# Issue order at three stage boundaries, and two steps from the sink attention's scores to its transposes

## The chip, the cores and the metric

The kernel runs on one core of a Trainium2 chip. The metric is the device time of one execution in microseconds (us), the median of a few runs. A core has five engines that each work through their own queue of instructions in order: TensorE (PE, with its weight loads as PEld), VectorE (DVE), ScalarE (ACT), GpSimd (POOL) and SyncE (SP). In this kernel SP issues the DMA transfers, so SP's queue is also the order in which loads and stores start.

## The reference

Three residual blocks over a sequence of 1024 tokens of width 1024, one after the other, all in f32.

```python
# block 1: dilated attention (3 groups of 8 heads) and an RWKV-7 recurrence side by side
proj = rms_norm(x, pre_norm_gain) @ w_in
y_attn = (o_attn * silu(z_attn)) @ w_up_attn
y_rwkv = (o_rwkv * silu(z_rwkv)) @ w_up_rwkv
merged = sigmoid(g_attn) * y_attn + sigmoid(g_rwkv) * y_rwkv
x1 = x + rms_norm(merged @ w_out, post_norm_gain)
# block 2: gMLP
u, v, z = split(rms_norm(x1, a_pre_g) @ a_w_in, 3)           # 2048 columns each
s = einsum('gts,bnsgc->bntgc', causal(w_s), layer_norm(gelu(v))) + b_s   # per 128-token chunk
x2 = x1 + rms_norm((gelu(u) * s * silu(z)) @ a_w_out, a_post_g)
# block 3: sliding-window attention, 16 query heads, 4 key/value heads, a sink in each softmax
kv_in = rms_norm(x2, kv_norm_g);  k = kv_in @ w_k;  v = kv_in @ w_v
q, z = split(rms_norm(x2, b_pre_g) @ b_w_in, 2)
m = maximum(max(logits + alibi), sink)
o = exp(logits - m) @ v / (sum(exp(logits - m)) + exp(sink - m))
out = x2 + rms_norm((o * silu(z)) @ b_w_out, b_post_g)
```

## The kernel before

**Products.** Each f32 operand is cut into a high and a low part (`whi`, `wlo`, `Ahi`, `Alo`: ACT copies the high part, DVE subtracts to get the low one), and a product is three products of such parts, summed in a bank of PSUM. A bank holds 128 x 512 f32. There are two pools of banks for this: `pd` has 2 slots, and `pb` (taken by `bank()`, `psP` too) has 6. A product that takes a slot waits until the slot's last user has been evacuated, that is, read by DVE or ACT.

**Order.** The order of the instructions on every engine is the order in which the program emits them (`manual_schedule`). A `tick` is called after every fourth matmul, and once more at a group's end. At a tick three things happen (`tick`): stores that were put on the list `late` with a count of ticks go out when the count of the list's head is used up (`store`, `flush`; the list is first in, first out); the weight planner (`w_step`) loads and splits weights as far as tiles are free; and each lane, a queue of generators, takes its next step, where `yield n` means that the next step comes n ticks on. `drain` and loops of the form `while ...: lane.step()` take steps at once.

**Phase 1 and 1a** compute block 1's projection, dilated attention (items of `att_unit`) and RWKV. **Phase 2**, the merge (`phase2`, `gated`), has 32 groups of 12 matmuls of 128 x 512: 16 on the RWKV branch (`or_hi`, `or_lo`), then 16 on the attention branch (`oa_hi`, `oa_lo`). Group n needs the gated activations of its half, which `gated` prepares: load `oa` and `ob`, multiply on DVE after 5 ticks (L1468), copy the high part on ACT (L1470), subtract on DVE (L1472). All 32 groups write to `pd`. Their evacuation is a DVE multiplication by a gate that is loaded two groups ahead (L1521).

**out_proj** is the output product with its residual, used as `w_out`, `a_out` and `b_out`. For each half of the tokens and each half c of the columns it keeps four banks, two of `pd` and then two of `pb`, as `ps[0]` to `ps[3]`, evacuated by ACT (L1635) and DVE (L1636). Afterwards `norm`, on lane `lane_n`, makes the residual sum, hands it to `store` with 3 ticks, and prepares the next block's activations.

**Phase 3** is block 2. Its products alternate between a bank of `pb` (`psP`) and one of `pd` (L1947). In the last round (`ct == 15`), after the third product, it flushes the late stores and sets up `a_out`, whose activations `stream` loads back from DRAM (`yraw<-Y`) and splits. `jit` starts the next split at a tick, as far as `jit_limit` allows; `jit_limit` 2 is set right there.

**Phase 4** is block 3. `swa_prep`, first on `lane_w`, issues the loads of the mask (`swa`), the slopes and, in four transfers, the sinks, and after 20 ticks lets POOL negate the sinks. The groups of v, k and the first two of q follow, then 14 more groups, q and z by turns, while `lane_a` runs the attention. An item of the attention is one of four steps d of a unit p:

- Q: score products (PE, L978)
- S: scores with bias and row minimum (DVE, L996), sinks (L1001), exponentials on ACT (L1008, L1011); scores go to the tiles `Sx`, exponentials to other tiles `P`
- norm: DVE adds the sink's term, inverts and scales P (L1022, L1024, L1028); only with sinks
- B: transposes of P on PE (L1042), copied by ACT (L1056 to L1058)
- C: products with V (L1077)

In a step of `att_unit`, C of the item two back comes first, then Q of the new item, B of the item before, S of the new one; 2 ticks later norm of the new one, and 3 ticks later the next step. Evacuations of a z group (`ev_z`) wait in the program until its unit's output is there (`while p not in self.Oh: self.lane_a.step()`), then emit `tz` on ACT (L2112), `tz` on DVE (L2113, L2114) and the split `yb` (L1495, L1496).

Of the kernel before, what the change touches and what calls it, by code (L numbers as in the profile page):

```python
# [129 lines left out]
class Core:  # L130
# [212 lines left out]
    def group(self, i, act, KT, half, evac, off=0):  # L343

        w = self.w_get(i)
        ps = self.pd.tile([128, 512], F32, tag="pd", name="pd")

        def op(k):
            wh, wl = w(k)
            ah, al = act(k, half)  # L350
            return wh[:, off:off + 128], wl[:, off:off + 128], ah, al
        self.mm(ps, KT, op)
        evac(ps, half)
        self.tick()
# [524 lines left out]
class Attn(Rwkv):  # L879
# [105 lines left out]
    def att_S(self, it):  # L985
# [4 lines left out]
        it["P"] = [self.s2("P") for _ in range(2)]  # L990
        Sx = [self.s2("Sx") for _ in range(2)]
# [22 lines left out]
    def att_norm(self, it):  # L1014

        nc = self.nc
        if "es" not in it:
            return
        es, d = it["es"], it["d"]
        e2 = es.rearrange("p (s j) -> p s j", s=2)  # L1020
        ST = it["u"]["ST"][:, 1].rearrange("p (s b) -> p s b", s=2)
        nc.vector.tensor_tensor(out=e2, in0=e2, in1=ST[:, :, 2 * d:2 * d + 2], op=ALU.add)  # L1022
        rd = self.sm.tile([128, 4], F32, tag="rd", name="rd", bufs=3)
        nc.vector.reciprocal(out=rd, in_=es)  # L1024
        for j in range(2):
            for s, c in enumerate(it["cols"][j]):
                P = it["P"][j]
                nc.vector.tensor_scalar(out=P[:, c], in0=P[:, c], scalar1=rd[:, 2 * s + j:2 * s + j + 1], scalar2=None,  # L1028
                                        op0=ALU.mult)
# [88 lines left out]
    def att_unit(self, u):  # L1118
        t = self.sm.tile([128, 32], F32, tag="ST", name="ST", bufs=3)
        u["STt"] = t  # L1120
        u["ST"] = t.rearrange("p (m s) -> p m s", m=2)
        for d in range(4):
            if len(self.pipe) > 1:
                self.att_C(self.pipe.pop(0))
            it = self.att_Q(u, d)
            if self.pipe:
                self.att_B(self.pipe[-1])
            self.att_S(it)
            self.pipe.append(it)
            yield self.pace[0]  # L1130
            self.att_norm(it)
            yield self.pace[1]

    def att_flush(self):
        while self.pipe:
            if "PT" in self.pipe[0]:
                self.att_C(self.pipe.pop(0))
            rest = [it for it in self.pipe if "PT" not in it]
            if rest:
                self.att_B(rest[0])  # L1140
            yield self.pace[0]
# [66 lines left out]
class Kernel(Attn):  # L1208
# [250 lines left out]
    def gated(self, o, sz, half, pr, h, l, x=None, done=None):  # L1459
# [7 lines left out]
        yield 5  # L1467
# [30 lines left out]
    def phase2(self):  # L1498
# [83 lines left out]
        for n in range(32):  # L1582
# [10 lines left out]
            self.group(i, act, 4, half, (ev_r if key == "r" else ev_a)(n), off=128 * (f % 2))  # L1593
# [8 lines left out]
    def out_proj(self, name, KT, post, xsrc, xdst, nxt, act):  # L1602
# [11 lines left out]
        def run(half, lanes):  # L1614
# [3 lines left out]
            for c in range(2):  # L1618
                i0 = self.first[name, half] + c * KP
                ps = [self.pd.tile([128, 512], F32, tag="pd", name="pd") for _ in range(2)] + [self.bank() for _ in range(2)]  # L1620
# [58 lines left out]
        def norm(half, og, x, ss):  # L1679
# [6 lines left out]
            for j in range(4):  # L1686
# [4 lines left out]
                self.store(xdst[128 * tt:128 * tt + 128, :], x[j], 3 if nxt is not None else 0)  # L1691
# [30 lines left out]
    def stream(self, src, KT, in_a):  # L1722
# [45 lines left out]

        self.jit = jit
# [80 lines left out]
    def phase3(self):  # L1850
# [105 lines left out]
        for ct in range(16):  # L1956
# [38 lines left out]
            self.tick()  # L1995
            c2 = add(product(i, combo("S2"), "T2"), c1)
            if ct:
                lane_s.add(spatial(ct, sp))
            if ct == 15:
                self.flush()  # L2000
                self.out2 = self.out_proj("a_out", 16, "a_post_g_2", self.X1, self.X2, "plain", self.stream(self.Y, 16, 4))
                self.jit_limit = 2
            self.tick()
# [29 lines left out]
    def swa_prep(self):  # L2033
        nc, I = self.nc, self.I
        t = self.s2("swa")
# [10 lines left out]
        yield 20  # L2046
# [144 lines left out]
```

## Time and profile before

| | |
|---|---|
| median of 3 runs | 2565.06 us (2563.25 to 2567.79) |
| profiled execution, its own time | 2560.33 us |
| its span in the trace | 2558.5 us |
| mean granted clock of TensorE | 0.984 |
| busy: PE, DVE, ACT, POOL | 96%, 49%, 39%, 23% of the span |
| DMA | 229.66 MB, mean 90 GB/s |

Times in the trace are us from the start of the span. A row of a timeline gives the start, the length and the instruction, and in brackets how long the engine had been idle and which instruction released it. `SPq` is the issue of a DMA. The granted clock is 1.00 at 2.4 GHz and 0.50 at 1.2 GHz. The profiled execution's own time holds 1.8 us that lie outside the span.

### The profile page before, as it was taken

The page shows a single profiled execution, that of the slowest core. Times are in us where ns is not written, and L with a number is a line of the kernel's source. Part 1 is how long each engine was busy: PE and PEld are TensorE (multiplying, and loading weights), DVE is VectorE, ACT ScalarE, POOL GpSimd, SP SyncE. Part 2 cuts the span into 40 slices and gives each one's busy share as a digit, 9 for nine tenths or more (in the row PEclk, how much of TensorE's full clock was granted, in tenths as well). Part 3 has the DMA queues.
Part 4 walks back from the last instruction along what each step waited for, and adds up shares of the span by engine and source line. Part 5 has one row for each costly group of instructions (what it writes and reads, how often), then busy time and mean ns, then how long its engine had stood idle before and what let it go on. Part 6 is the DMA issues. An engine that isn't in the chain of part 4 may idle for free.

```text
span 2558.5 us, 39497 instructions
## 1 busy us (share of the span) xinstructions
PE 2464.2 (96%) x15058; PEld 1944.8 (76%) x15058; DVE 1262.5 (49%) x3010; ACT 1009.4 (39%) x2583; POOL 599.4 (23%) x885
## 2 busy tenths in 40 slices
PE   7999999999999999999999999999999997999998
PEld 5767777777777777777788777888877886777777
DVE  5445545453322323235647347655555546566545
ACT  4222222222244444454235232544443433466632
POOL 0161715234000102011410135544440004000000
PEclk9999999999999999999999999999999999999999
DMA  5321201111211213137734232332335544000033
GB/s 144 72 59 38 71 27 57 47 54 54 50 51 30 75 45 75 46 79 225 239 113 182 87 109 85 99 99 78 100 99 201 188 133 127 26 26 26 18 115 141
DMA packets 247666, 229.66 MB, mean 90 GB/s; under 512 B 25035, under 2 KB 188939, under 8 KB 247476
## 3 DMA queue, kind: packets, MB, share of 16 engines
q1 hardware_dynamic: 247476, 227.13, 29.1%
q8 instruction: 119, 1.95, 0.3%
q14 instruction: 71, 0.58, 0.1%
HBM read 179.61 MB, written 47.48 MB: 89 GB/s over the span
## 4 chain that ended last, share of the span: by engine, by line
PE 61%; DVE 6%; DMA 4%; ACT 4%; issue 2%; POOL 2%; SPq 0%; DVEq 0%; ACTq 0%; POOLq 0%
PE pd L336 31%; PE pb L1628 7%; PE pd L1628 7%; PE pd L1947 4%; PE psP L1947 3%; PE psO L1077 2%; PE pb L1042 2%; PE pb L978 2%; DMA vg<-Vd 2%; DVE wlo L278 1%; PE pb L1926 1%; ACT vg L1905 1%; ACT P L1008 1%; DVE wlo L1496 1%; DMA gate<-GT 1%
## 5 line engine op out<-in xcount | busy, mean ns | idle before, releaser
L336 PE MATMUL pd<-Ahi,whi 128*128 128x512 f32 x1488 | 598.8, 402 | 21.3 <-DVE K L2079 12.7
L336 PE MATMUL pd<-Ahi,wlo 128*128 128x512 f32 x1488 | 598.1, 402 | 0.7 <-DVE wlo L278 0.7
L336 PE MATMUL pd<-Alo,whi 128*128 128x512 f32 x1488 | 597.5, 402 | 0.6 <-DVE Alo L427 0.6
L336 PEld LDWEIGHTS pd<-Ahi,whi 128*128 128x128 f32 x1488 | 283.3, 190 | 84.9 <-issue 17.8
L278 DVE TENSOR_TENSOR wlo<-wraw,whi 128x512 fp32r<-128x512 f32 x380 | 270.4, 748 | 150.3 <-ACT whi L277 142.8
L336 PEld LDWEIGHTS pd<-Alo,whi 128*128 128x128 f32 x1488 | 283.1, 190 | 62.3 <-issue 4.0
L336 PEld LDWEIGHTS pd<-Ahi,wlo 128*128 128x128 f32 x1488 | 282.8, 190 | 60.8 <-issue 2.1
L277 ACT ACTIVATE whi<-wraw 128x512 fp32r<-128x512 f32 x380 | 217.2, 621 | 58.5 <-POOL wraw L271 14.3
L1008 ACT ACTIVATE P<-Sx,ST 128x192 f32<-128x192 f32 (+2 forms) x320 | 130.5, 410 | 8.2 <-DVE ST L996 4.4
L1496 DVE TENSOR_TENSOR wlo<-wraw,whi 128x512 fp32r<-128x512 f32 x96 | 82.1, 869 | 56.8 <-ACT whi L1495 56.8
L996 DVE CUSTOM_DVE_ANT_0 Sx<-pb,BT 128x64 f32<-128x64 f32 (+1 forms) x192 | 44.6, 287 | 130.7 <-PE pb L978 130.3
L336 PE MATMUL pd<-wlo,Ahi 128*128 128x512 f32 x256 | 100.5, 393 | 2.5 <-DVE wlo L278 2.5
L336 PE MATMUL pd<-whi,Ahi 128*128 128x512 f32 x256 | 100.2, 391 | 0.0
L336 PE MATMUL pd<-whi,Alo 128*128 128x512 f32 x256 | 100.1, 391 | 0.0
L723 POOL TENSOR_TENSOR X<-UC,X 128x60 f32<-128x60 f32 (+24 forms) x248 | 79.5, 320 | 57.9 <-DVE UC L716 40.0
L725 POOL TENSOR_TENSOR X<-X 128x60 f32<-128x60 f32 (+24 forms) x248 | 79.4, 320 | 19.4
L1495 ACT ACTIVATE whi<-wraw 128x512 fp32r<-128x512 f32 x96 | 59.6, 622 | 58.4 <-POOL wraw L223 54.5
L271 POOL TENSOR_TENSOR wraw<-wraw,bpg 128x1024 f32<-128x1024 f32 x16 | 31.1, 1952 | 210.6 <-DMA wraw<-in_b_w_in_dram 154.3
L1042 PE MATMUL pb<-K,P 128*128 128x128 f32 (+1 forms) x388 | 63.2, 291 | 15.4 <-DVE P L1028 15.4
L1077 PEld LDWEIGHTS psO<-PT,V 128*64 128x64 f32 x1040 | 55.1, 136 | 28.3 <-issue 21.6
L1077 PE MATMUL psO<-PT,V 128*64 128x128 f32 x1040 | 74.4, 280 | 0.0
L1905 ACT ACTIVATE vg<-vg,lnv 128x128 f32<-128x128 f32 x128 | 52.6, 482 | 47.3 <-DMA vg<-Vd 47.3
(416 smaller groups left out, 4823.8 us busy)
## 6 DMA issues: line engine op xcount, KB each, us to landing
wraw<-in_w_in_dram SPq DMA_DIRECT2D x78, 512.0 KB
wraw<-in_a_w_in_dram SPq DMA_DIRECT2D x48, 512.0 KB
wraw<-in_a_w_out_dram SPq DMA_DIRECT2D x32, 512.0 KB
GT<-gt SPq DMA_DIRECT2D x32, 256.0 KB
gate<-GT SPq DMA_DIRECT2D x32, 256.0 KB
wraw<-in_w_out_dram SPq DMA_DIRECT2D x16, 512.0 KB
X<-xr SPq DMA_DIRECT2D x16, 512.0 KB
Vd<-v SPq DMA_DIRECT2D x32, 256.0 KB
```

The source lines that it names most:

```text
L277: nc.scalar.activation(out=his[j], in_=t[:, s], func=AF.Copy)
L278: nc.vector.tensor_tensor(out=los[j], in0=t[:, s], in1=his[j].bitcast(F32), op=ALU.subtract)
L336: nc.tensor.matmul(ps, lhsT=a, rhs=b, start=(n == 0), stop=(n == last))
L723: nc.gpsimd.tensor_tensor(out=tv, in0=U[:, j:j + 1, 0:j].to_broadcast([128, w, j]), in1=X[:, b0:8, j:j + 1].to_broadcast([128, w, j]), op= ...
L725: nc.gpsimd.tensor_tensor(out=X[:, b0:8, 0:j], in0=X[:, b0:8, 0:j], in1=tv, op=ALU.add)
L1008: nc.scalar.activation(out=it["P"][j][:, c], in_=Sx[j][:, c], func=AF.Exp, scale=-1.0, bias=ST[:, 0, n:n + 1], accum_out=ST[:, 1, n:n + 1])
L1042: tr = lambda x, m=128: nc.tensor.transpose(ps[0:m, 128 * x:128 * x + 128], Pt[:, 128 * x:128 * x + m], self.ident)
L1077: nc.tensor.matmul(O(h).rearrange("p (s x) -> p s x", s=2), lhsT=V[:, b - 1 + t, c:c + 64], rhs=rhs, start=t == tiles[0], stop=t == 1)
L1496: nc.vector.tensor_tensor(out=lo, in0=src, in1=hi.bitcast(F32), op=ALU.subtract)
L1628: nc.tensor.matmul(ps[j], lhsT=a, rhs=b, start=(k == 0 and n == 0), stop=(k == KT - 1 and n == 2))
L1905: nc.scalar.activation(out=v[:, tt, :], in_=v[:, tt, :], func=AF.Identity, scale=lnv[:, tt, 1:2], bias=lnv[:, tt, 0:1])
L1947: nc.tensor.matmul(ps, lhsT=a, rhs=b, start=(n == 0), stop=(n == 11))
```

## The change

At the three boundaries between the blocks:

- **Merge** (`group`, `phase2`, `gated`): every odd group writes to a bank of `pb` (`other=True`) and not of `pd`. `gated` waits 7 ticks between its loads and its first multiplication, where it waited 5.
- **out_proj**: `ps[0]` and `ps[1]` are of `pb`, `ps[2]` and `ps[3]` of `pd`. The stores of the residual sums go out 14 ticks after they are handed over, where it was 3 (`b_out` still stores at once).
- **a_out loads** (`stream`, `phase3`): `stream` issues the first two loads when it is set up (`ahead=2`), which now comes before the third product of the last round; the flush there is gone; `jit_limit = 2` is set after the tick that follows.
- **Mask constants** (`swa_prep`): the loads of mask, slopes and sinks go out after 24 ticks; the negation follows 10 ticks later.

In the sink attention, B of an item comes two steps after its S, and not one, so that the pipe is one item longer: norm of an item is emitted in the next item's step, at the place where the new item's norm was. The exponentials are written over the scores, so that `Sx` and `P` are the same tiles. For the dilated attention, which has no sinks, the order stays, and the tiles are shared as well.

```diff
--- before.py
+++ after.py
@@ -340,10 +340,10 @@
             if after is not None:
                 after(k)
 
-    def group(self, i, act, KT, half, evac, off=0):
+    def group(self, i, act, KT, half, evac, off=0, other=False):
 
         w = self.w_get(i)
-        ps = self.pd.tile([128, 512], F32, tag="pd", name="pd")
+        ps = self.bank() if other else self.pd.tile([128, 512], F32, tag="pd", name="pd")
 
         def op(k):
             wh, wl = w(k)
@@ -987,8 +987,8 @@
         nc = self.nc
         u, d, ps = it["u"], it["d"], it.pop("ps")
         BT, ST = u["bias"], u["ST"]
-        it["P"] = [self.s2("P") for _ in range(2)]
-        Sx = [self.s2("Sx") for _ in range(2)]
+
+        it["P"] = Sx = [self.s2("P") for _ in range(2)]
         for s in range(2):
             for j in range(2):
                 c, nk = it["cols"][j][s], it["nk"][j][s]
@@ -1016,7 +1016,7 @@
         nc = self.nc
         if "es" not in it:
             return
-        es, d = it["es"], it["d"]
+        es, d = it.pop("es"), it["d"]
         e2 = es.rearrange("p (s j) -> p s j", s=2)
         ST = it["u"]["ST"][:, 1].rearrange("p (s b) -> p s b", s=2)
         nc.vector.tensor_tensor(out=e2, in0=e2, in1=ST[:, :, 2 * d:2 * d + 2], op=ALU.add)
@@ -1119,16 +1119,19 @@
         t = self.sm.tile([128, 32], F32, tag="ST", name="ST", bufs=3)
         u["STt"] = t
         u["ST"] = t.rearrange("p (m s) -> p m s", m=2)
+
+        n = 2 if "nsink" in u else 1
         for d in range(4):
-            if len(self.pipe) > 1:
+            if len(self.pipe) > n:
                 self.att_C(self.pipe.pop(0))
             it = self.att_Q(u, d)
-            if self.pipe:
-                self.att_B(self.pipe[-1])
+            if len(self.pipe) >= n:
+                self.att_B(self.pipe[-n])
             self.att_S(it)
             self.pipe.append(it)
             yield self.pace[0]
-            self.att_norm(it)
+            if n == 2 and len(self.pipe) > 1:
+                self.att_norm(self.pipe[-2])
             yield self.pace[1]
 
     def att_flush(self):
@@ -1137,6 +1140,7 @@
                 self.att_C(self.pipe.pop(0))
             rest = [it for it in self.pipe if "PT" not in it]
             if rest:
+                self.att_norm(rest[0])
                 self.att_B(rest[0])
             yield self.pace[0]
 
@@ -1464,7 +1468,7 @@
         if x is None:
             nc.sync.dma_start(a, o[pr][:, s])
         nc.sync.dma_start(b, sz[pr][:, s])
-        yield 5
+        yield 7
         nc.vector.scalar_tensor_tensor(out=a, in0=a if x is None else x[:, s], scalar=0.5, in1=b, op0=ALU.mult, op1=ALU.mult)
         yield 1
         nc.scalar.activation(out=h, in_=a, func=AF.Copy)
@@ -1590,7 +1594,7 @@
                 self.lane_g.step()
             gate(n + 2)
             i = self.first[key] + f // 2
-            self.group(i, act, 4, half, (ev_r if key == "r" else ev_a)(n), off=128 * (f % 2))
+            self.group(i, act, 4, half, (ev_r if key == "r" else ev_a)(n), off=128 * (f % 2), other=n % 2 == 1)
             if f % 2 and half:
                 self.w_free(i)
         mg_split()
@@ -1617,7 +1621,7 @@
             ss = self.sm.tile([128, 2, 4], F32, tag="oss", name="oss")
             for c in range(2):
                 i0 = self.first[name, half] + c * KP
-                ps = [self.pd.tile([128, 512], F32, tag="pd", name="pd") for _ in range(2)] + [self.bank() for _ in range(2)]
+                ps = [self.bank() for _ in range(2)] + [self.pd.tile([128, 512], F32, tag="pd", name="pd") for _ in range(2)]
 
                 def part(kp, j):
                     w = self.w_get(i0 + kp)
@@ -1688,7 +1692,7 @@
                 for h in range(2):
                     xs = x[j][:, 512 * h:512 * h + 512]
                     nc.vector.scalar_tensor_tensor(out=xs, in0=og[h, j], scalar=r[:, j:j + 1], in1=xs, op0=ALU.mult, op1=ALU.add)
-                self.store(xdst[128 * tt:128 * tt + 128, :], x[j], 3 if nxt is not None else 0)
+                self.store(xdst[128 * tt:128 * tt + 128, :], x[j], 14 if nxt is not None else 0)
                 yield 1
                 if nxt is not None:
                     for h in range(2):
@@ -1719,7 +1723,7 @@
 
         return run
 
-    def stream(self, src, KT, in_a):
+    def stream(self, src, KT, in_a, ahead=0):
 
 
 
@@ -1766,6 +1770,8 @@
                 split()
             return hl[half, k]
 
+        for _ in range(ahead):
+            load()
         self.jit = jit
         return act
 
@@ -1993,14 +1999,16 @@
             self.tick()
             c5 = copy(product(i, combo("S1"), "T1"), "c5")
             self.tick()
+            if ct == 15:
+
+                actY = self.stream(self.Y, 16, 4, 2)
+                self.out2 = self.out_proj("a_out", 16, "a_post_g_2", self.X1, self.X2, "plain", actY)
             c2 = add(product(i, combo("S2"), "T2"), c1)
             if ct:
                 lane_s.add(spatial(ct, sp))
+            self.tick()
             if ct == 15:
-                self.flush()
-                self.out2 = self.out_proj("a_out", 16, "a_post_g_2", self.X1, self.X2, "plain", self.stream(self.Y, 16, 4))
                 self.jit_limit = 2
-            self.tick()
             z0 = gate(add(product(i, block(0, 1), "B21"), c1, c1))
             u0 = self.s2("u0")
             nc.gpsimd.tensor_tensor(out=u0, in0=c2, in1=c5, op=ALU.add)
@@ -2032,6 +2040,7 @@
 
     def swa_prep(self):
         nc, I = self.nc, self.I
+        yield 24
         t = self.s2("swa")
         nc.sync.dma_start(t[:, 0:384], I["const_swa"].rearrange("p a k -> p (a k)"))
         sl = self.const.tile([128, 2, 8], F32, name="slope")
@@ -2043,7 +2052,7 @@
             for s in range(2):
                 nc.sync.dma_start(self.sink[64 * h:64 * h + 64, s, :],
                                   I["b_sinks_2"].rearrange("o (p h) -> h o p", h=2)[h ^ s].to_broadcast([64, 8]))
-        yield 20
+        yield 10
         nc.gpsimd.tensor_scalar(out=self.nsink, in0=self.sink, scalar1=-1.0, scalar2=None, op0=ALU.mult)
         self.swa_t, self.swa_sl = t, sl
         yield 1
```

## Rows read from the trace of the kernel before

**Rows 1.** The page: busy us by engine; shares of the chain of waits

```profile
PE 2464.2 (96%) x15058; PEld 1944.8 (76%) x15058; DVE 1262.5 (49%) x3010; ACT 1009.4 (39%) x2583; POOL 599.4 (23%) x885
...
PE 61%; DVE 6%; DMA 4%; ACT 4%; issue 2%; POOL 2%; SPq 0%; DVEq 0%; ACTq 0%; POOLq 0%
```

**Rows 2.** Waits of TensorE: instruction, releaser: us in total, times, longest

```profile
PE pb L1042 <- DVE P L1028: 15.4, 10, 3.0
PE pd L336 <- DVE K L2079: 12.7, 2, 11.0
PE pd L1628 <- DVE sum L1967: 6.3, 2, 4.5
...
PE pd L336 <- DVE m L1521: 4.5, 4, 2.0
PE pd L336 <- ACT gt L1361: 4.0, 1, 4.0
```

**Rows 3.** Stretches: length, busy us (count) by engine, PEclk, DMA share, GB/s

```profile
1199.60:1255.00 55.40, 46.91 (x182) 37.00 (x182) 38.03 (x54) 13.02 (x23) 13.72 (x5) 0.91 0.92 295
1203.70:1209.90 6.20, 6.20 (x15) 4.84 (x16) 5.24 (x12) 1.15 (x2) 0.00 (x0) 0.50 0.75 280
2112.00:2132.00 20.00, 20.00 (x90) 16.57 (x89) 13.25 (x38) 11.02 (x30) 4.15 (x4) 1.00 0.08 11
2132.00:2169.70 37.70, 24.62 (x115) 19.53 (x113) 25.43 (x29) 11.47 (x22) 21.47 (x11) 0.86 0.69 202
2200.00:2450.00 250.00, 234.62 (x1805) 180.94 (x1805) 150.83 (x602) 160.72 (x583) 13.28 (x7) 0.98 0.09 26
```

**Rows 4.** Chain of waits from a_out into phase 4

```profile
2115.07 2.73 PE pb L1628 x12
...
2128.68 13.46 DMA wraw<-in_b_w_in_dram
```

**Rows 5.** Timeline of TensorE in the merge (start, length, instruction, [idle before])

```profile
1203.70 0.79 PE L336 MATMUL pd<-or_hi,whi 128*128 128x512 f32 x1 [4.03 <-ACT gt L1361]
...
1254.82 0.39 PE L336 MATMUL pd<-oa_hi,whi 128*128 128x512 f32 x1
```

**Rows 6.** Chain of waits over the merge (start us, us, what)

```profile
1229.55 8.22 DMA gate<-GT
...
1238.72 0.69 DVE m L1521
```

**Rows 7.** Timeline of VectorE at the end of a_out

```profile
2117.19 0.69 DVE L1636 TENSOR_TENSOR og<-pb,row 128x512 f32<-128x512 f32 x1 [0.67 <-ACT junk L1635]
```

**Rows 8.** Chain of waits over the start of a_out

```profile
1920.18 5.54 DMA yraw<-Y
...
1932.15 2.29 DVE wlo L278 x2
...
1937.69 0.69 DVE sum L1967
```

**Rows 9.** Timeline of SyncE (DMA issues) at the same boundary

```profile
2113.03 2.71 SPq L2044 DMA_DIRECT2D sink<-in_b_sinks_dram  x4
2122.96 5.62 SPq L168 DMA_DIRECT2D X<-xr  x4
2128.68 8.47 SPq L204 DMA_DIRECT2D wraw<-in_b_w_in_dram  x2
```

**Rows 10.** DMA packets between 2112 and 2132 us

```profile
DMA packets 2198, 0.21 MB, mean 11 GB/s; under 512 B 2070, under 2 KB 2198, under 8 KB 2198
```

**Rows 11.** Timeline of VectorE in the sink attention, before the longest wait

```profile
2345.29 0.69 DVE L2113 SCALAR_TENSOR_TENSOR tz<-tz,pd 128x512 f32<-128x512 f32 x1 [2.45 <-ACT tz L2112]
...
2347.39 2.22 DVE L1496 TENSOR_TENSOR yb<-tz,yb 128x512 fp32r<-128x512 f32 x1 [0.69 <-ACT yb L1495]
2349.53 0.15 DVE L1022 TENSOR_TENSOR es<-es,ST 128x4 f32<-128x4 f32 x1
```

**Rows 12.** Timeline of VectorE in the sink attention, at another wait

```profile
2232.39 0.16 DVE L1022 TENSOR_TENSOR es<-es,ST 128x4 f32<-128x4 f32 x1 [2.27 <-ACT es L1011]
```

## The prediction

> **What bounds the kernel now.** I read the page first. TensorE is busy 96% of the span and holds 61% of the chain of waits [rows 1]: only its idle time and its clock are left to win, and a shorter DVE or ACT instruction is worth what it takes off a wait of TensorE. So the next view was the waits of TensorE [rows 2]. The boundaries hold 4.0 us (merge, for the evacuation `gt`) and 4.5 (merge, `m`), 6.3 (start of `a_out`, `sum`) and 12.7 (phase 4, `K`). The sink attention holds 15.4 in ten waits for `P`. The third view, stretches, gives the clock beside them [rows 3]: 0.91 in the merge, 0.86 behind 2132 us, 0.98 in the sink attention. At 0.50, 15 matmuls took 6.20 us [rows 3]; at full clock 12 take 2.73 [rows 4], so 15 take 3.4. A dip of that length costs 2.8 us beside the wait ahead of it.
>
> **Merge.** From 1199.6 to 1255.0 TensorE is busy 46.9 of 55.4 us [rows 3]. Group 0 ends at 1199.67 and group 1 starts at 1203.70 [rows 5], though groups n and n+1 have different slots of `pd`: the slot of group 1 was last used by phase 1a, and its evacuation stands on ACT behind a copy that waits for DVE. The first group of the attention branch, n = 16, starts at 1254.82. Between them 15 groups are 15 x 2.73 = 41.0 us, so nothing could start n = 16 before 1240.7: at most 14.1 us to win. With odd groups on six more slots, group 1 needs no old slot. Group 2 is the first to meet the occupied slot, at 1199.67 + 2.73 = 1202.4, and waits 1.3 us for 1203.70. Later waits for `m` (4.5 in all) go, because TensorE can stand about four groups ahead of the evacuation and not two. What is late next is the gates: DMA is busy 0.92 of this stretch at 295 GB/s [rows 3], and a gate issued at 1229.55 lands 8.22 us later, at 1237.8 [rows 6]. DVE then evacuates, from 1238.72 on [rows 6], what are the tenth and eleventh of these evacuations: group 9 and, by 1239.5, group 10, whose slot group 14 needs. Two groups of 2.73 later n = 16 could start, at 1245.0. I allow 2.3 us for a later gate: 1247.3, a gain of 7.5. Bounds: 2 (only the wait at 1203.70, less the 1.3 of group 2) and 10. The 2 ticks more in `gated` hide behind the same lead.
>
> The granted clock in this stretch falls to 0.50 just behind the 4.03 us wait [rows 3, 5]. The Trainium skill ("TensorE: Matmul & The Clock Gate", HAM oscillation, how this bites in real kernels) tells of a kernel that waits for DMA where more PSUM buffers gave no further gain, and in the next section of cycling through PSUM banks that itself makes the clock swing. By that rule the merge gains nothing; that result is weighed below as the first rival.
>
> **out_proj's order of banks.** At the end of an output product the next group takes `pd`. With `pd` last in the order its slot was that of j = 2, whose DVE evacuation, if it stays where it is, ends at 2117.19 + 0.69 = 2117.88 [rows 7], against matmuls of j = 3 that end at 2115.07 + 2.73 = 2117.80 [rows 4]. I take 0.3 us lost at each of two such ends: -0.6 (bounds -1.2 and 0). At the start of `a_out` the same order is part of the next gain.
>
> **a_out loads.** The read-back is issued at 1920.18 and lands 5.54 us later [rows 8]. ACT and DVE, which work in order, stand at its split, and the evacuations behind are late, so that TensorE waits 1.8 and 4.5 us [rows 2] and then runs a dip. The new place is a product earlier in the program, but on SP the store of the last round stays ahead of the loads, so they start only some 0.5 us earlier; emitting the split a tick later moves one pair of weight splits ahead of it. I put the evacuations 1.2 us earlier (0.5 + 0.7 of one split on DVE). With `pb` first, TensorE also does j = 0 and 1 of the first step (2 x 6 matmuls, 2.7 us) before it meets `pd`. The `sum` that it needs still ends at about 1938.4 - 1.2 = 1937.2 [rows 8], because two `wlo` (2.29 us) and POOL's work stand ahead of it. So of 6.3 us of waits some 3.5 remain: gain 2.8, and 0.7 from a shorter dip: 3.5. Bounds 0 (wait moved) and 9.1 (6.3 and all of a dip of 2.8).
>
> **Phase 4's boundary.** The longest wait, 11.0 us of the 12.7, is for `K`, but `K` is the last link: DVE is held by `wlo` of `b_w_in`, whose load was issued at 2128.68 and landed 13.46 us later, at 2142.14 [rows 4]. Why so late? SP issues in order [rows 9]: the sinks at 2113.03, then the four residual stores, which wait for DVE until 2122.96 and take 5.62 us, and only then the loads. Meanwhile DMA did almost nothing: 11 GB/s, 2198 packets, 2070 of them under 512 B [rows 3, 10], which is the sinks, read element by element (128 x 16 = 2048). Nothing that was issued behind them moved until about 2132, 19 us after them.
>
> After the change the loads of `b_w_in` stand ahead of both: the planner can emit them at ticks 9 and 15, the stores come at 14 ticks and the constants after 24. They then land before 2124, and the wait of 11.0 goes, with 1.7 us of the other `K` wait and the half clock behind the long one, which I estimate at ten matmuls of (6.20 - 3.4) / 15 = 0.19 us lost each, 1.9 [rows 3, 4]: 14.6, less 0.4 for a wait that remains: 14.2. The sinks are not gone. At 24 ticks (about 2117.6 + 24 x 0.9 = 2139) their 19 us fall on 2139 to 2158, where one weight load (second half of `K`) stands behind them. It is needed by about 2161, and the negation on POOL may wait ahead of a weight gain. I take 0.7 us (0 to 6). Net 13.5, from 8 to 15.
>
> **Sink steps.** Ten waits, 15.4 us. The longest, 3.0, ends with `norm` at 2349.53, which stood on DVE behind `tz`, itself 2.45 us late because its ACT partner stands behind the exponentials, and behind `yb`, 2.22 us long [rows 11]. `norm` waited for nothing itself. In nine of ten waits it is so; only the one at 2232.39 shows `norm` waiting for the exponentials (2.27) [rows 12]. Now `norm` of the older item is emitted at the very place where `norm` of the new one was, 3 ticks ahead of its transposes, and behind the same `tz` and `yb`. An older item doesn't move it up DVE's queue. So the wait stays in nine cases; 1.3 us go in one, and the pipe's extra item at the end of the attention takes about as much: 0. Bounds: -3 and +20 (all 15.4, and 2% of 250 us at 0.98).
>
> **Residual stores** at w_out and the shared tiles: SP had no loads that TensorE waits for near w_out's end; 0.
>
> **Sum.** 7.5 - 0.6 + 3.5 + 13.5 + 0 = 23.9 us, from 2560.33 (span and 1.8 around it) to 2536.4. The median of the runs is 4.7 above the profiled execution; on it, 2565.1 - 23.9 = 2541. A measurement can tell about 0.2% (5 us) from no change.
>
> **Rivals.**
> - *A gain is only moved* (0.21). Either the merge is bound by DMA (0.92 busy speaks for it; that the longest wait there ends with an evacuation on ACT and not with a gate [rows 2], against) and wins nothing: 23.9 - 7.5 = 16.4, 2549. Or the sinks' 19 us meet a load at their new place and cost half of 13.5: 17, 2548. Both: 2555.
> - *The sink steps do what a longer pipe can* (0.15): if what counts is how long ago the exponentials were, all ten waits go: 20 us more, 2521. For it: TensorE waits for `P` only. Against: the nine of ten [rows 11].
> - *Slower* (0.06): the longer pipe makes an output ready one step later, and `ev_z` has to force steps. One forced step sets `tz` behind a whole item on ACT and DVE: 3.0 us like the longest wait, and half a dip of 2.8: 4.4. At all eight units it is 35, so 2541 + 35 = 2576. By the count of ticks (20 per unit, 24 per pair of groups) only the first unit is late, and the slack grows by 4 ticks a unit. It decides above five units: 24 / 4.4.
> - *Nothing* (0.05): the queues land in the same order, because slots and not emission hold the loads back: 2561 to 2569.
>
> **How the numbers follow.** The likeliest has 0.53; its own range goes from 2531 (the upper bounds, 10 + 9.1 + 15 = 34.1 without the sink steps' 20) to 2550 (half way to the lower bounds, whose sum is 5.8). The range for 8 in 10 takes in most of the first two rivals: 2520 to 2556. Faster by over 0.2% (under 2560): 0.53 + 0.20 + 0.15 = 0.88; within: 0.01 + 0.05 = 0.06; slower: 0.06.
>
> **What would show it.** Right: the waits `gt` and `m` at the merge shrink to about 2 to 3 us and `oa_hi` starts near 1247; `b_w_in` is issued before the stores, and there is no wait over 2 us for `K`; the ten waits for `P` stay at 12 to 16 us. Wrong: a new wait behind the constants at 2139 to 2165 (a `wraw` or `nsink`), waits for `P` under 5 us, or a wait at z groups for `Oh`. Any of the last three would move the time out of the likeliest range.

## The result, and the profile after

The changed kernel runs in 2531.2 us (median of 4, 2528.7 to 2542.8) against 2564.2 for the kernel before on the same chip (median of 4): a ratio of 0.988 with a 95% interval of 0.985 to 0.992. In a later comparison (4 runs against 9) it was 2541.8 against 2565.7, 0.989 (0.988 to 0.991). The forecast was 2541, 23.9 us under the median before; the two comparisons give 33 and 24. The profiled execution took 2528.7 us with a span of 2526.9, against 2560.3 and 2558.5.

One span against one span misleads here. The order of the matmuls of 512 columns is the same in all kernels of this study, so each stage can be measured between the starts of the same two matmuls, whatever happened ahead of it. The first half of the merge, for instance, runs from an anchor, the last matmul but one of group 0 (1199.05 in the kernel before, 1196.21 in the changed one), to the first matmul with `oa_hi` (1254.82 and 1243.14). "Old form" takes in every profile, of the experiments below too, whose code is as before in that stage; "as changed" every one whose code is there as in the changed kernel. Worked out from the traces in this way, us:

| stage | old form: mean (range, profiles) | as changed: mean (range, profiles) | gain | forecast |
|---|---|---|---|---|
| start to the merge (only the shared tiles differ) | 1203.1 (1199.1 to 1206.7, 7) | 1200.8 (1196.0 to 1205.9, 6) | - | - |
| merge, first half | 53.7 (52.9 to 55.8, 5) | 47.5 (46.5 to 48.8, 6) | 6.2 | 7.5 |
| end of w_out | 12.0 (12.0, 6) | 12.5 (12.4 to 12.5, 8) | -0.5 | -0.3 |
| start of a_out | 74.6 (72.7 to 75.5, 5) | 70.7 (68.3 to 72.6, 7) | 3.9 | 3.5 |
| end of a_out, head of phase 4 | 44.5 (44.4 to 44.5, 4) | 34.6 (33.2 to 36.0, 6) | 9.9 | 13.5 - 0.3 |
| sink attention | 301.6 (300.1 to 303.6, 7) | 296.0 (295.4 to 296.4, 3) | 5.6 | 0 |
| sum | | | 25.1 | 23.9 |

The first line is the lesson in reading spans: ahead of the merge profiles differ by 11 us. The profile shown below is the earliest of its kind at that point but one (1196.2). Of the 31.6 us by which its span is shorter, 2.8 lie ahead of the merge and 28.8 in the stages of the table, 3.7 more than the sum of the means. In the start of `a_out` the two ranges nearly touch (72.6 and 72.7).

The page of the changed kernel, busy time and chain of waits, which answers to [rows 1]:

```profile
PE 2456.4 (97%) x15058; PEld 1938.9 (77%) x15058; DVE 1260.2 (50%) x3010; ACT 1009.0 (40%) x2583; POOL 598.0 (24%) x885
...
PE 66%; DVE 5%; ACT 3%; DMA 2%; POOL 1%; issue 1%; SPq 0%; DVEq 0%; ACTq 0%; POOLq 0%
```

TensorE's share of the chain goes from 61% to 66%. The waits of TensorE in the changed kernel (us in total, times, longest), which answer to [rows 2]:

```profile
PE pb L1042 <- DVE P L1028: 12.4, 8, 4.2
PE pd L336 <- DVE wlo L278: 5.9, 6, 3.0
...
PE pd L336 <- ACT or_hi L1474: 2.5, 2, 1.3
PE pb L1632 <- ACT y_hi L1499: 1.9, 1, 1.9
PE pd L1953 <- DVE sum L1973: 1.5, 1, 1.5
```

The waits for `K`, `m` and for `sum` at the start of `a_out` are gone, and `gt` is down to 0.2. New are one of 2.95 for `wlo`, two for `or_hi` and one for `y_hi`. The ten waits for `P` are now eight. Stretches of the changed kernel that answer to those of [rows 3] (length, busy us and count by engine, granted clock, DMA share, GB/s): the merge's first half, the head of phase 4, the first 250 us of the sink attention:

```profile
1196.40:1243.14 46.74, 43.83 (x182) 34.94 (x182) 39.84 (x54) 13.34 (x24) 13.74 (x5) 0.96 0.98 307
...
2114.00:2151.80 37.80, 34.16 (x160) 27.51 (x159) 22.02 (x43) 12.53 (x24) 5.22 (x4) 0.95 0.31 80
2172.00:2422.00 250.00, 237.02 (x1830) 182.55 (x1829) 146.51 (x605) 160.97 (x584) 13.28 (x7) 0.98 0.09 27
```

The merge's clock is 0.96, and TensorE idles 2.9 of 46.7 us where it idled 8.5 of 55.4. At the boundary, SyncE's timeline (start, length, transfer) answers to [rows 9]:

```profile
2063.28 4.07 SPq L204 DMA_DIRECT2D wraw<-in_b_w_in_dram  x2
2105.71 0.34 SPq L168 DMA_DIRECT2D X<-xr  x1
...
2124.72 2.70 SPq L2053 DMA_DIRECT2D sink<-in_b_sinks_dram  x4
2127.52 1.72 SPq L204 DMA_DIRECT2D wraw<-in_w_k_dram  x1
```

`b_w_in` is issued at 2063, far ahead of the stores, and not near tick 9: the order in SyncE's queue decides, and SyncE runs ahead of TensorE until an instruction has to wait. In the kernel before, that instruction was the load of the mask, which SyncE issued at 2112.16 after 31 us without an issue (30.4 of them a wait for TensorE's matmuls of `a_out`), and everything stood behind it.

### The profile page after: what moved, and what is told of

Same layout as the page of the kernel before. It is cut to its first block, busy times and chain, and to the rows that moved or that the text cites. A ratio compares the mean times of both kernels' runs of the same rounds, so it can differ in the third digit from the quotient of the medians.

```text
span 2526.9 us, 39417 instructions
## 1 busy us (share of the span) xinstructions
PE 2456.4 (97%) x15058; PEld 1938.9 (77%) x15058; DVE 1260.2 (50%) x3010; ACT 1009.0 (40%) x2583; POOL 598.0 (24%) x885
## 4 chain that ended last, share of the span: by engine, by line
PE 66%; DVE 5%; ACT 3%; DMA 2%; POOL 1%; issue 1%; SPq 0%; DVEq 0%; ACTq 0%; POOLq 0%
PE pd L336 31%; PE pb L1632 7%; PE pd L1632 7%; PE pd L1953 5%; PE psP L1953 5%; PE psO L1077 2%; PE pb L1042 2%; PE pb L978 2%; PE pb L336 2%; PE pb L1932 1%; DMA vg<-Vd 1%; DVE wlo L278 1%; ACT P L1008 1%; PE psT L423 1%; PE pb L954 0%
## 5 line engine op out<-in xcount | busy, mean ns | idle before, releaser
L1008 ACT ACTIVATE P<-P,ST 128x192 f32<-128x192 f32 (+2 forms) x320 | 130.5, 410 | 8.0 <-DVE ST L996 4.8
L996 DVE CUSTOM_DVE_ANT_0 P<-pb,BT 128x64 f32<-128x64 f32 (+1 forms) x192 | 44.5, 287 | 130.5 <-PE pb L978 130.0
L1042 PE MATMUL pb<-K,P 128*128 128x128 f32 (+1 forms) x388 | 61.6, 287 | 12.4 <-DVE P L1028 12.4
L1911 ACT ACTIVATE vg<-vg,lnv 128x128 f32<-128x128 f32 x128 | 52.6, 482 | 46.5 <-DMA vg<-Vd 46.5
L1056 ACT COPY PT<-pb 128x256 f32<-128x256 f32 x100 | 37.0, 370 | 83.2 <-PE pb L1042 83.0
```

The lines of the kernel that those rows point to most:

```text
L1008: nc.scalar.activation(out=it["P"][j][:, c], in_=Sx[j][:, c], func=AF.Exp, scale=-1.0, bias=ST[:, 0, n:n + 1], accum_out=ST[:, 1, n:n + 1])
L1042: tr = lambda x, m=128: nc.tensor.transpose(ps[0:m, 128 * x:128 * x + 128], Pt[:, 128 * x:128 * x + m], self.ident)
```

## Experiments

Each kernel's place in the stages is told, since one span says little (the merge alone, e4, has a span of 2558.7, 0.2 us over the kernel before, and a merge that is 8.8 us shorter: its start was late by 7.6, and other stages, which its edits don't touch, took 1.4 longer). e4 to e9 have one run each, so their times give no verdict (e5 to e8: 2558.6, 2559.8, 2553.1 and 2566.5 us, beside one run of the kernel before at 2568.3), and a stage of theirs is one profile against the ranges of the table.

**Norm ahead of S (e1).**

```diff
+            if n == 2 and self.pipe:
+                self.att_norm(self.pipe[-1])
             self.att_S(it)
             self.pipe.append(it)
             yield self.pace[0]
-            if n == 2 and len(self.pipe) > 1:
-                self.att_norm(self.pipe[-2])
```

> The changed kernel, with norm of the older item emitted ahead of S of the new item, 2 ticks earlier and ahead of tz and yb on VectorE. Theory A (the waits for P come from norm's place in VectorE's queue, behind tz, yb and weight splits): the waits for P, 12.4 us in the changed kernel, fall below 4, the dips of the clock behind them go too, and the span falls by 8 to 15 us from 2526.9. Theory B (the waits come from the age of the exponentials or from work on ScalarE): the waits stay at 10 to 14 us and the span within 3 us of 2526.9.

Measured: sink attention 285.4 us against 296.3 in the changed kernel's profile. No wait for `P` is left. The span is only 2.6 us under the changed kernel's, where 8 to 15 were expected, and the median, 2530.0 (4 runs), 1.2 under: in this profile the stages that the edit doesn't touch took 8.3 us longer. The comparison on one chip below (e10, e11) shows the gain in the time as well. The waits of TensorE in that stretch, first of the changed kernel, then of its second profile with norm early (e11):

```profile
PE pb L1042 <- DVE P L1028: 12.4, 8, 4.2
PE psO L1077 <- ACT PT L1057: 0.5, 1, 0.5
```

```profile
PE psO L1077 <- ACT PT L1057: 4.9, 2, 4.4
```

Theory A holds: the waits come from norm's place in VectorE's queue. What comes next is one wait of 4.4 us for ScalarE's copy of the transposes (`PT`). VectorE in the changed kernel, ahead of the longest wait (TensorE's transposes start at 2411.92, 4.15 us late), shows the same pattern as [rows 11]:

```profile
2407.13 0.69 DVE L278 TENSOR_TENSOR wlo<-wraw,whi 128x512 fp32r<-128x512 f32 x1 [2.02 <-ACT whi L277]
2407.74 0.68 DVE L2122 SCALAR_TENSOR_TENSOR tz<-tz,pd 128x512 f32<-128x512 f32 x1
...
2409.84 0.69 DVE L1500 TENSOR_TENSOR yb<-tz,yb 128x512 fp32r<-128x512 f32 x1 [0.69 <-ACT yb L1499]
2410.45 0.68 DVE L278 TENSOR_TENSOR wlo<-wraw,whi 128x512 fp32r<-128x512 f32 x1
2411.05 0.16 DVE L1022 TENSOR_TENSOR es<-es,ST 128x4 f32<-128x4 f32 x1
```

The line at 2411.05 has no bracket: norm's first instruction waits for nothing, and so it is at all eight waits that the changed kernel has for `P`. Ahead of it stand a weight split that waited 2.02 us for ScalarE, then `tz`, `yb` and another split.

**One step again (e2).**

```diff
-        n = 2 if "nsink" in u else 1
+        n = 1
...
-            if n == 2 and len(self.pipe) > 1:
-                self.att_norm(self.pipe[-2])
+            self.att_norm(it)
...
-                self.att_norm(rest[0])
                 self.att_B(rest[0])
```

> The changed kernel with one step between scores and transposes again; scores and exponentials still share tiles. Theory A (two steps with norm at the old place buy little): the sink attention, from the start of the first later group of q to b_out, is 2 to 5 us longer than in the changed kernel (3.7 us lie between the kernel before and the changed one there), with waits for P of 14 to 17 us. Theory B (the second step is what counts): 8 us or more longer. If the shared tiles made the 3.7 us, it is 0 to 1 us longer.

Measured: sink attention 301.8, waits for `P` 14.9 us, median 2544.8. It is 5.5 us over the changed kernel's first profile, a little more than theory A's 2 to 5, and equal to the old form's mean (301.6). So the second step carries the gain, and the shared tiles carry nothing that shows beside the old form's spread (300.1 to 303.6).

**5 ticks (e3), the merge alone (e4), 7 ticks alone (in e9).**

```diff
-        yield 7
+        yield 5
```

> The changed kernel with 5 ticks and not 7 between gated's loads and its first multiplication. If the 7 ticks matter: the two waits of 1.33 and 1.13 us for or_hi near 1207 change, and the first oa_hi group starts 2 us or more later or earlier than 1243.1. If the banks make the whole gain of the merge (8.8 us between the two kernels): it starts within 1 us of 1243.1.

Measured: 51.3 us, 4.4 over the changed kernel's first profile and 2.5 over the longest of the six with 7 ticks (48.8); the median was 2541.0 (4 runs). So the ticks matter, which the prediction had at nothing. VectorE with 5 ticks, then with 7 (bracket: idle before, releaser):

```profile
1213.30 0.69 DVE L1525 SCALAR_TENSOR_TENSOR m<-gate,pd 128x512 f32<-128x512 f32 x1
1218.06 1.19 DVE L1472 SCALAR_TENSOR_TENSOR oa<-oa,ob 128x512 f32<-128x512 f32 x1 [4.07 <-DMA ob<-SZA]
...
1220.56 0.68 DVE L1525 SCALAR_TENSOR_TENSOR m<-gate,pb 128x512 f32<-128x512 f32 x1
...
1226.26 2.49 DVE L1472 SCALAR_TENSOR_TENSOR oa<-oa,ob 128x512 f32<-128x512 f32 x1 [2.01 <-DMA ob<-SZA]
```

```profile
1214.10 0.68 DVE L1525 SCALAR_TENSOR_TENSOR m<-gate,pd 128x512 f32<-128x512 f32 x1
...
1217.30 1.07 DVE L1472 SCALAR_TENSOR_TENSOR oa<-oa,ob 128x512 f32<-128x512 f32 x1 [1.73 <-DMA ob<-SZA]
1218.29 0.68 DVE L1525 SCALAR_TENSOR_TENSOR m<-gate,pb 128x512 f32<-128x512 f32 x1
...
1229.50 0.68 DVE L1472 SCALAR_TENSOR_TENSOR oa<-oa,ob 128x512 f32<-128x512 f32 x1
```

The multiplication waits for `ob`, a load in a stretch where DMA is busy 0.98, and the evacuations `m` queue behind it. The same five evacuations stand ahead of the first multiplication shown in both runs, and VectorE stands there 1.73 us and not 4.07. The last one shown, two multiplications on, has eight evacuations ahead of it with 7 ticks, and seven with 5: there VectorE stands not at all, against 2.01 us. With 5 ticks TensorE pays later:

```profile
1200.68 0.50 PE L336 MATMUL pd<-or_hi,whi 128*128 128x512 f32 x1 [1.40 <-ACT gt L1365]
...
1233.48 0.77 PE L336 MATMUL pd<-or_hi,whi 128*128 128x512 f32 x1 [4.04 <-DVE m L1525]
```

> The kernel before with the merge's two edits alone (odd groups on pb, 7 ticks). If the merge's gain is its own: the start of the first oa_hi group comes 8 to 10 us earlier against the end of the first merge group, and the span is 8 to 10 us under 2558.5. If it is bound by DMA: 0 to 3 us.

e4 is the kernel before with `other=n % 2 == 1` and `yield 7`. Measured: 46.9 us, 8.8 under the profile before and 6.8 under the mean of the old form; of the waits for `m` and `gt` 0.2 us is left there. The merge's gain is its own, and DMA did not bind the old form. The fourth combination is e9, with 7 ticks on the old banks and, in another stage, the new order of banks:

```diff
-        yield 5
+        yield 7
...
-                ps = [self.pd.tile(...) for _ in range(2)] + [self.bank() for _ in range(2)]
+                ps = [self.bank() for _ in range(2)] + [self.pd.tile(...) for _ in range(2)]
```

> The kernel before with two edits that act in different stages: 7 ticks in gated with all merge groups still on pd, and out_proj's order of banks (pb first) with the old a_out loads. Merge: if 7 ticks help only an engine that can run ahead, the first half of the merge stays at 52.5 to 54 us; if they help by themselves, it falls to 48 to 50. a_out, to the start of its second half's columns: with the loads alone 72.4 us and in the kernel before 74.5 to 75.4; if the order of banks carries as much as the loads it comes to 71 to 73, if it carries nothing 74 to 75.

Measured: merge 52.5 us, against 53.7. Banks alone 2.4 us, ticks alone 1.2, both 6.2. The first two rest on one profile each, and 52.5 is only 0.4 under the lowest of the old form (52.9). TensorE's waits for `m` and `gt` say it more plainly: 8.7 us with the ticks alone, where the old form has 7.7 to 8.5, 5.4 with the banks alone, and 0.2 to 0.4 with both, beside 2.4 to 2.5 for `or_hi`, which are new. So in e9 the ticks by themselves took no wait away, and the banks need them for the larger part of their gain. In the start of `a_out` the order alone gives 73.5, within the old form's range (72.7 to 75.5). The run's time, 2567.2, is no verdict: one run, with a start at 1205.

**The boundary: constants late (e5), stores late (e6), sinks by row (e7),** each on the kernel before.

```diff
+        yield 24
         t = self.s2("swa")
...
-        yield 20
+        yield 10
```

> The kernel before with the mask, slopes and sinks loaded 24 ticks later and nothing else. The changed kernel gains 10 us at this boundary. Theory A (the element-wise sinks stop everything behind them for 19 us): the residual stores still stand ahead of b_w_in on SyncE, but move at once, b_w_in lands near 2133 and not 2142, and the 11.0 us wait for K falls to 1 to 3 us. Theory B (the place of the stores ahead of the loads is what counts): it stays above 7 us.

```diff
-                self.store(xdst[...], x[j], 3 if nxt is not None else 0)
+                self.store(xdst[...], x[j], 14 if nxt is not None else 0)
```

> The kernel before with the residual stores after 14 ticks and nothing else. Theory A (sinks): the loads are issued near 2115 and yet land only when the sinks are through, at 2134 to 2136, so the wait for K falls to 3 to 5 us. Theory B (stores): it falls below 1 us.

```diff
-        for h in range(2):
-            for s in range(2):
-                nc.sync.dma_start(self.sink[64 * h:64 * h + 64, s, :], ...to_broadcast([64, 8]))
+        sr = t[:, 384:400]
+        nc.sync.dma_start(sr, I["b_sinks_2"].to_broadcast([128, 16]))
         yield 20
+        for h in range(2):
+            for s in range(2):
+                nc.gpsimd.tensor_copy(out=self.sink[64 * h:64 * h + 64, s, :],
+                                      in_=sr[64 * h:64 * h + 64, :].rearrange("q (p h) -> q h p", h=2)[:, h ^ s, :])
```

> The kernel before with the sinks loaded as one row of 16 values to each partition (128 packets of 64 B), in place of 2048 packets of 4 B, and put in order by four small copies on GpSimd after the same 20 ticks; all places in the order stay. Theory A (packets): as with the constants late, b_w_in lands near 2133 and the wait for K falls to 1 to 3 us. Theory B (the order on SyncE): it stays above 7 us.

Measured, head of phase 4: constants late 38.1 us, stores late 39.2, sinks by row 35.8, all edits 34.6, none 44.5. SyncE in e6 and in e7:

```profile
2116.09 2.70 SPq L2044 DMA_DIRECT2D sink<-in_b_sinks_dram  x4
2118.89 15.61 SPq L204 DMA_DIRECT2D wraw<-in_b_w_in_dram  x2
2134.59 5.08 SPq L168 DMA_DIRECT2D X<-xr  x1
```

```profile
2113.63 0.42 SPq L2043 DMA_DIRECT2D swa<-in_b_sinks_dram  x1
2123.57 4.30 SPq L168 DMA_DIRECT2D X<-xr  x4
2127.96 1.49 SPq L204 DMA_DIRECT2D wraw<-in_b_w_in_dram  x2
```

In e6 the loads are issued behind the sinks, and their issue alone takes 15.61 us; the wait for `K` falls to 7.5 us, not to the 3 to 5 that theory A gave nor below 1 as theory B did. In e7 everything keeps its place, stores first, and the same issue takes 1.49 us; the wait for `K` is gone and one of 3.2 for `wlo` stands in its place. The packets of 4 bytes are the cause: without them, with the order on SyncE as before, 35.8 us are left, within the range of all edits (33.2 to 36.0). (e7 also has one transfer for the sinks and not four; the two are not told apart.) `b_w_in` was issued at 2129 in e5, 2119 in e6 and 2128 in e7: only in the changed kernel, which has both moves, is it issued at 2063. With the constants late the wait for `K` goes too, but one of 6.5 us for `wlo` takes its place, where 1 to 3 were expected for `K`. VectorE and GpSimd of e5 there:

```profile
2133.85 6.60 DVE L1708 TENSOR_SCALAR og<-xr,or 128x512 f32<-128x512 f32 x4
2140.37 4.79 DVE L278 TENSOR_TENSOR wlo<-wraw,whi 128x512 fp32r<-128x512 f32 x5
```

```profile
2134.04 4.09 POOL L271 TENSOR_TENSOR wraw<-wraw,bpg 128x1024 f32<-128x1024 f32 x2 [15.97 <-DMA wraw<-in_b_w_in_dram]
2138.09 4.11 POOL L271 TENSOR_TENSOR wraw<-wraw,kvg 128x1024 f32<-128x1024 f32 x2
```

The four `og` of the norm stand ahead of the split on VectorE, and beside GpSimd's gains they take 6.60 us; in e7 they take 3.32 and in the changed kernel 1.67. The waits for `wlo` in the three are 6.5, 3.2 and 2.95 us. Late constants freed the loads, and the loads brought the gains beside the norm.

**a_out loads alone (e8).**

```diff
+            if ct == 15:
+                actY = self.stream(self.Y, 16, 4, 2)
+                self.out2 = self.out_proj("a_out", ..., actY)
             c2 = add(product(i, combo("S2"), "T2"), c1)
             ...
-            if ct == 15:
-                self.flush()
-                self.out2 = self.out_proj("a_out", ..., self.stream(self.Y, 16, 4))
-                self.jit_limit = 2
             self.tick()
+            if ct == 15:
+                self.jit_limit = 2
```

> The kernel before with the a_out loads ahead of the third product, no flush there, and the later jit_limit, but with the old order of banks. The changed kernel gains 6.7 us at this start. If the earlier loads make it: they land 3 us or more earlier against TensorE's products, the two waits for sum (6.3 us) fall below 3 us, and the start of a_out gains 4 to 7 us. If the order of banks makes it: waits of 4 to 6 us stay and the gain is 0 to 3 us.

Measured: 72.4 us, a gain of 2.2 on the mean of the old form, and 0.3 under its lowest. One wait for `sum` is left, of 4.3 us, and with the order of banks alone (e9) one of 4.4 as well:

```profile
PE pd L1628 <- DVE sum L1969: 4.3, 1, 4.3
```

```profile
PE pd L1628 <- DVE sum L1967: 4.4, 1, 4.4
```

In the seven profiles with both, `sum` costs 0 to 1.7 us. So each edit takes away the shorter of the two waits, and the long one goes only with both; the 2.2 us of the loads alone and the 1.1 of the order alone are not told from the spread.

**The changed kernel and norm early once more (e10, e11), and a last version (e12).**

> The changed kernel once more, for its stages in a second profile and beside the next two on the same chip. Stages as in its first profile: the first half of the merge 46 to 48.5 us, phase 4 up to the second half's groups 33 to 36, sink attention 294 to 297.

> The changed kernel with norm ahead of S, again, beside the changed kernel on the same chip. Theory A gave a sink attention of 285.4 us against 296.3, so the median should be 8 to 12 us under the changed kernel's. If the gain is lost to the other stages, as the first medians (2530.0 and 2531.2) would have it, it is within 3 us.

> The changed kernel with norm ahead of S, 9 ticks in gated in place of 7, and the sinks loaded by row at their late place. Expected beside the run before it: the merge's first half within 1.5 us (9 ticks take away the last waits for ob on VectorE, or bring waits for or_hi), and 0 to 1 us from the sinks, since TensorE waited for nothing behind them in the changed kernel.

e12 is e1 with `yield 9` in `gated` and, at the late place, the sinks by row as in e7. Measured on one chip: e10 2541.8 us (4 runs), e11 2528.2 (4), e12 2533.3 (5); ratios to the kernel before 0.989 (0.988 to 0.991), 0.984 (0.982 to 0.986) and 0.986 (0.984 to 0.988). e11 beats both kernels: its sink attention is 284.2 us against 296.4, 12.2 less, of the 13.6 between the medians. e10, the changed kernel again, repeats the head of phase 4 and the sink attention (34.8 and 296.4), but its merge takes 48.8 us and not 46.9, the start of `a_out` 72.6 and not 68.3, and its way to the merge 1205.9, 9.7 more.

In e12 the merge reads 44.7 us, 2.6 under e11's, but that doesn't show that 9 ticks are better than 7: a wait that no run with 7 ticks has there now lies in group 0, just ahead of the anchor.

```profile
1206.49 0.50 PE L336 MATMUL pd<-or_lo,whi 128*128 128x512 f32 x1 [1.95 <-DVE or_lo L1476]
```

From the first matmul of group 0, e12 takes 49.3 us and e11 49.7. What follows the head of phase 4 rises from 38.5 to 41.5, because of the sinks, where 0 to 1 us of gain were expected. VectorE and GpSimd of e12 there:

```profile
2143.72 2.13 DVE L278 TENSOR_TENSOR wlo<-wraw,whi 128x512 fp32r<-128x512 f32 x1
2145.77 4.16 DVE L1712 TENSOR_SCALAR og<-xr,or 128x512 f32<-128x512 f32 x2
2149.85 2.38 DVE L278 TENSOR_TENSOR wlo<-wraw,whi 128x512 fp32r<-128x512 f32 x1
```

```profile
2141.55 3.75 POOL L271 TENSOR_TENSOR wraw<-wraw,kvg 128x1024 f32<-128x1024 f32 x2
2145.26 8.72 POOL L271 TENSOR_TENSOR wraw<-wraw,bpg 128x1024 f32<-128x1024 f32 x4
```

In the changed kernel GpSimd waits for the sinks until 2148, and its gains run later. Here they start 21 us earlier against the same matmuls, and while they run two `og` take 4.16 us and a `wlo` 2.38 (in the changed kernel at 2130 to 2132: 0.88 for two `og`, 0.69 for one `wlo`). TensorE waits 1.36 us for `og`.

## Why the prediction was right

The time, its sign and most of the sum were right. Two terms were not, phase 4 (3.3 us too much) and the sink steps (5.6 too little), and it is luck that their errors have opposite signs: without it the sum would not have come within 1.2 us of the 25.1 in the table.

- **Merge, 7.5 forecast, 6.2 measured.** The mechanism held: group 1 starts at once, TensorE runs ahead, the first `oa_hi` starts 46.9 us after the anchor. But that the 2 ticks "hide behind the same lead" was wrong: with 5 ticks only 2.4 of the 6.2 remain. The step looked at TensorE's lead and not at VectorE's order, in which a multiplication waits for a load ahead of evacuations. What came late next was not a gate, for which 2.3 us were allowed, but `or_hi`. One reading was 0.5 us early: the trace has the evacuation of group 10 end at 1239.99, and not by 1239.5. The rival that the merge gains nothing fell. The Trainium skill ("TensorE: Matmul & The Clock Gate", HAM oscillation, how this bites in real kernels) reports that PSUM double-buffering gave a kernel no further gain, after its loop had been changed so that it does more matmuls before it waits for DMA; it states no rule for a kernel like this one. Here, with DMA busy 0.98, more banks gave 6.2 us with the load's wait moved as well and 2.4 without.
- **Order of banks, -0.3 a place: -0.5** at the end of w_out.
- **a_out, 3.5 forecast, 3.9 measured.** The size was right, but not what it is made of. The forecast left 3.5 us of waits for `sum`; `sum` costs 0 to 1.7 us with both edits, and 1.9 to 2.8 us for `y_hi`, of a later read-back, is what came next. That the two edits need each other, as e8 and e9 show, was not foreseen.
- **Phase 4, 13.5 less 0.3 forecast, 9.9 measured.** The chain from the sinks through SyncE to `K` was right, and e7 shows it by itself. The term was too large because the prediction priced what came late next at 0.4 us. It is `wlo` behind VectorE's norm chain: 2.95 us, and behind it about eight matmuls at half clock, 0.43 us apart and not 0.23, 1.6 us in all. VectorE and GpSimd in the changed kernel there:

```profile
2115.64 1.82 DVE L386 SCALAR_TENSOR_TENSOR nt_b<-nt_a,ms 128x4 f32<-128x4 f32 x1
...
2117.68 1.67 DVE L1712 TENSOR_SCALAR og<-xr,or 128x512 f32<-128x512 f32 x4
2119.27 0.68 DVE L278 TENSOR_TENSOR wlo<-wraw,whi 128x512 fp32r<-128x512 f32 x1
```

```profile
2115.54 1.90 POOL L271 TENSOR_TENSOR wraw<-wraw,kvg 128x1024 f32<-128x1024 f32 x1 [2.34 <-DMA wraw<-in_w_v_dram]
```

  An instruction of 128x4 that takes 0.16 us elsewhere took 1.82 while GpSimd ran a gain, and four `og` stood behind it. The sinks' stall was placed at 2139; it came at 2125 to 2144, and TensorE waited for nothing behind it, so the 0.7 us set aside for that were not spent.
- **Sink steps, 0 forecast, 5.6 measured.** That most of the waits stay while norm keeps its place was right (12.4 of 15.4 us stay, and e1 takes them all away by moving norm), and so was that the one wait in which norm stood for the exponentials goes. "The pipe's extra item takes about as much" was wrong, and so was the claim that only 1.3 us can go: in the seven profiles of the old form the waits for `P` are 14.8 to 17.6 us, in the three as changed 12.3 to 12.5, and the longest before, 2.97, is not among them. The 4.15 us at the end of the attention are no price of the second step: three of the seven old ones have 4.1 to 4.2 there too. Of the 5.6 us, 3.3 are idle time of TensorE and the rest is busy time, at a granted clock of 0.98 to 0.99. Why these waits and not others went is not settled.
- **Residual stores at w_out: 0, and nothing there moved**: phase 3 begins at the same distance but for the order of banks.
- The slower rival did not occur: no z group waits for its output.

## What to carry to other kernels

When an engine that works in order makes another one wait, a deeper pipe does only part of the work; the late instruction has to move up in its engine's queue as well. Here the second step gave 5.6 us, and moving norm ahead of S 11 to 12 more. Two edits can also need each other: at the merge and at the start of `a_out` the long waits went only with both. In a queue of transfers, count packets and not bytes: 8 KB of constants in 4-byte packets held back a megabyte of weights. And ask what a freed transfer or engine starts earlier: in e5 and e12 GpSimd's gains, no longer held back, slowed VectorE on the path.

## What the runs showed of the hardware

2048 packets of 4 bytes took 19 us, about 110 in a microsecond, with next to nothing else moving in that time in the kernel before and in the changed one (11 and 10 GB/s). The changed kernel's packets from 2123 to 2145 us, which answer to [rows 10]:

```profile
DMA packets 2291, 0.22 MB, mean 10 GB/s; under 512 B 2156, under 2 KB 2291, under 8 KB 2291
```

Two profiles of the changed kernel differ by 9.7 us in the first 1200 us of the span. The first has 34 us at half clock there, and the second (e10) 51; 17 us at half clock lose up to 8.5 us of work, most of the difference. VectorE instructions are 3 to 11 times longer beside GpSimd's gains (`wlo` 0.69 to 2.38, the 128x4 instruction 0.16 to 1.82). The Trainium skill ("SBUF — State Buffer", Who interferes with whom) calls the port pair that the two engines share an exclusive lock, which one instruction holds for its whole length. The rows agree: the 1.82 us end, as the gain of 1.90 us does, at 2117.4 to 2117.5.
